# Loading order, constant matmuls and the issue order of a convolution's first stage in a two-layer decoder trunk

## The chip, the cores and the metric

The kernel runs on one core of one Trainium2 chip. The metric is the device time of one execution in microseconds (us). Before the change three runs took 1135.62, 1135.75 and 1136.22 us; the median is 1135.75 us.

A core has five engines with instruction queues of their own, each executed in order: TensorE (PE, matmuls; its weight loads are shown apart as PEld), VectorE (DVE), ScalarE (ACT), GpSimd (POOL) and SyncE (SP, which here only issues DMAs). They wait for one another through semaphores.

## What is computed

Two layers over 512 tokens of 1024 channels, in float32. The part that the change touches is the first half of layer 0; the rest follows behind it.

```python
h = x + conformer_conv(rmsnorm(x, norm_mix[0]), ...)      # layer 0
h = h + swiglu_ffn(rmsnorm(h, norm_ffn[0]), ...)
# shared K/V, windowed attention with sinks, output projection, second SwiGLU, final rmsnorm

def conformer_conv(x, w_pw1, b_pw1, w_dw, b_dw, ln_g, ln_b, w_pw2, b_pw2):
    a = jax.nn.glu(x @ w_pw1 + b_pw1, axis=-1)            # 1024 -> 2 x 1024
    y = depthwise_causal_conv(a, w_dw) + b_dw             # 31 taps for each channel
    y = jax.nn.silu(layernorm(y, ln_g, ln_b))             # statistics over the channels
    return y @ w_pw2 + b_pw2
```

## The kernel before

**Layout and order of the stages.** Activations lie with channels on the partitions: `h` is eight tiles (ct 0 to 7) of 128 channels by 512 tokens. Layer 0 works in two halves of 256 tokens (`HALF[0]`, `HALF[1]`). The first stage runs, for each half and each ct, the first pointwise projection (`Pw1`, two groups of eight f32 matmuls of 128x128 by 128x256, L535: linear part and gate part), the GLU gate (`gate`: a sigmoid on ACT, L544 or L547, and a product on DVE, L549, into the padded tile `apad`), and the 31 taps of the depthwise conv. Then come layer norm and silu (`rows`, the tile `z`), the second projection (`pw2`, L252, f32), and the FFN (`ffn_part`). From the FFN on a weight is split into a high and a low part (L202 on ACT, L203 on DVE) and each product takes three matmuls (L254 to L256). The conv of the second half of the tokens runs beside `pw2` and the FFN of the first half.

**Loads.** SP issues in program order: the first half of the tokens in four pieces of 256 KB (L279), both 512 KB pieces of the first projection weight `w1[0]` (L283), the tap weights `wdw` (L288), the second half of the tokens, then `w1[1]` to `w1[7]`, and later the stream of all other weights in chunks of 512 KB (L186).

**The first norm.** ACT squares the eight token tiles (L321), POOL adds them (L325), TensorE sums over the channels (`step1`, L335), DVE and POOL make the reciprocal root (L337, L339), ACT puts it on a diagonal (L347), and TensorE spreads it over all partitions with a matmul by ones (`spread`, L360). The first `N_RAW` = 2 projections use tokens that are scaled by the gain alone (L510 on DVE, `raw`) and are multiplied by the reciprocal root afterwards in `gate` (L546, L548); the others wait for `norm_x` (L517 on DVE), which writes normalised tokens `xg`.

**The conv.** A class `Half` holds one half. `taps` makes the taps of one ct: the first `TAPS - n_pool` ones on DVE (L582, L584), the last `n_pool` as a product on ACT (L574, L576, into a ring of eight tiles `pr`) and a running sum on POOL (L577); a last POOL add joins both (L587). `N_POOL` says how many go to POOL, for each half and each pair of tiles. `conv` walks over pairs of tiles, one step being one DVE tap of both with the ACT and POOL taps that fall to it. `shift_rows` (L604) makes a common shift from the first pair by two matmuls, which DVE adds (L611). `squares` (L613, ACT) and `sums` (L622, four matmuls by ones for each pair) gather the layer norm's statistics. `scales` copies them (L627, ACT), makes rows (L630, TensorE), mean and reciprocal root (L632, L639), and diagonals (L644, ACT); `spread` (L648) spreads them; `rows` makes `z` (L660, L661 on DVE, L662 on ACT).

**What sets the order of the work.** The tile framework schedules: it takes the program's order as a priority and puts each engine's instructions in a fixed order when the program is built, hoisting what is ready. `tc.issue_after(ins)` holds what is issued inside it behind an instruction. The hand-written part is a loop over the 14 projections that are left after the first two (`projs`, index `at_`): after projection `at_` the conv of the first half is advanced so that it is done at `at_` = 11, the entries of `follow` place statistics (`squares` at 4, 6, 9, 11, `sums` one later, `scales` at 12), and `spread` stands between the two halves of the last projection. At `at_` = 12 the second half's conv is begun with `N_EARLY` = 10 steps (L733 ff.). What is left of it is a paced job: `pace` spreads its steps evenly over the next 44 weight chunks (those of `pw2` and of the FFN's first part).

## Time and profile before

| | us |
|---|---|
| median of three runs | 1135.75 |
| the profiled execution | 1136.61 |
| its span in the profile | 1134.8 |
| TensorE matmul busy, of the span | 1104.5 (97%) |
| TensorE weight loads busy | 961.7 (85%) |
| DVE busy | 666.1 (59%) |
| ACT busy | 513.3 (45%) |
| POOL busy | 341.4 (30%) |
| mean granted clock of TensorE | 0.995 |

The span runs from the first to the last instruction in the record; the execution's time is taken around it and is 1.8 us longer. Busy shares are means over the whole span: in the first 250 us, where the conv runs, DVE, ACT and POOL are much busier than here. The rows of a timeline give start and length in us, engine, line, operation, output and inputs, shape and count, and in square brackets the idle time before and what ended it. One f32 matmul appears as two records. The rows of a stretch `A:B` give its length, then for PE, PEld, DVE, ACT and POOL busy time with the number of instructions begun in brackets, then the granted TensorE clock, the mean busy share of the DMA engines and GB/s.

### The profile page before, as it was taken

The numbers are of one execution on the slowest core, as the hardware profiler recorded it, in microseconds if no ns is written. First come the engines' busy times: TensorE is split into PE (matmuls) and PEld (weight loads), VectorE is DVE, ScalarE is ACT, GpSimd is POOL, SyncE is SP. The second block draws the span as 40 slices with busy tenths as digits, with TensorE's granted clock in tenths as the row PEclk, the third lists the DMA queues.
The fourth block names the chain that finished last, engine by engine and source line by source line (L and its number), as shares of the span: only waits on it lengthen the run. The fifth ranks groups of instructions, "written<-read, shape, count | busy, mean of one in ns | idle before, by whom it ended". The sixth has DMA issues, their size and how long they took to land.

```text
span 1134.8 us, 16051 instructions
## 1 busy us (share of the span) xinstructions
PE 1104.5 (97%) x6126; PEld 961.7 (85%) x6126; DVE 666.1 (59%) x1071; ACT 513.3 (45%) x898; POOL 341.4 (30%) x437
## 2 busy tenths in 40 slices
PE   6999999899999999999999999999999999999997
PEld 5888789899999998888878778888888888888886
DVE  3998748897876643454464675764454333444455
ACT  2786887744654432232352574653332222222234
POOL 2997989921011001121220242332111100110014
PEclk9999999999999999999999999999999999999998
DMA  9380044456555552223323211113323332233232
GB/s 358 112 95 1 0 149 149 130 188 237 171 188 184 186 186 93 93 93 108 96 75 106 81 38 38 38 56 109 96 93 94 102 101 93 93 99 104 95 97 89
DMA packets 41577, 128.16 MB, mean 113 GB/s; under 512 B 4475, under 2 KB 12828, under 8 KB 41500
## 3 DMA queue, kind: packets, MB, share of 16 engines
q1 hardware_dynamic: 40924, 126.69, 35.9%
q8 instruction: 48, 0.79, 0.3%
q10 hardware_dynamic: 576, 0.44, 0.1%
q14 instruction: 29, 0.24, 0.1%
HBM read 121.87 MB, written 5.24 MB: 112 GB/s over the span
## 4 chain that ended last, share of the span: by engine, by line
PE 84%; POOL 5%; DVE 4%; issue 3%; ACT 3%; DMA 0%; SPq 0%; POOLq 0%; ACTq 0%; DVEq 0%
PE bank L254 24%; PE bank L255 24%; PE bank L256 24%; PE bank L535 8%; POOL pr L577 3%; PE bank L864 1%; DVE wlo L203 1%; DVE quad L368 1%; PE bank L885 1%; ACT whi L202 1%; ACT pr L576 1%; PE bank L622 1%; DVE bank L584 1%; DMA h<-in_xT_dram 0%; ACT z L662 0%
## 5 line engine op out<-in xcount | busy, mean ns | idle before, releaser
L255 PE MATMUL bank<-quad,whi 128*128 128x512 f32 (+1 forms) x1584 | 543.4, 343 | 2.0 <-DVE quad L368 2.0
L256 PE MATMUL bank<-quad,wlo 128*128 128x512 f32 (+1 forms) x1584 | 542.4, 343 | 2.4 <-DVE wlo L203 2.4
L254 PE MATMUL bank<-quad,whi 128*128 128x512 f32 (+1 forms) x1584 | 543.0, 344 | 0.2
L203 DVE TENSOR_TENSOR wlo<-raw,whi 128x1024 fp32r<-128x1024 f32 x200 | 272.6, 1363 | 316.8 <-ACT whi L202 306.2
L202 ACT CAST whi<-raw 128x1024 fp32r<-128x1024 f32 x200 | 209.3, 1048 | 338.4 <-PE bank L255 295.8
L255 PEld LDWEIGHTS bank<-quad,whi 128*128 128x128 f32 x1584 | 300.7, 190 | 37.6 <-DVE quad L368 2.7
L256 PEld LDWEIGHTS bank<-quad,wlo 128*128 128x128 f32 x1584 | 300.2, 190 | 38.1 <-DVE wlo L203 3.4
L254 PEld LDWEIGHTS bank<-quad,whi 128*128 128x128 f32 x1584 | 300.4, 190 | 36.5 <-ACT quad L903 0.6
L445 POOL TENSOR_TENSOR tmp<-tmp,tmp 128x512 f32<-128x512 f32 x32 | 45.6, 1426 | 426.7 <-DVE tmp L444 412.2
L577 POOL TENSOR_TENSOR pr<-pr,pr 128x256 f32<-128x256 f32 x208 | 158.6, 798 | 7.5 <-ACT pr L576 6.5
L535 PE MATMUL bank<-quad,w 128*128 128x256 f32 x512 | 116.4, 388 | 8.4 <-DMA w<-in_W_dram 8.4
L535 PEld LDWEIGHTS bank<-quad,w 128*128 128x128 f32 x512 | 99.2, 195 | 23.3 <-DVE quad L510 8.3
L576 ACT ACTIVATE pr<-apad,wdw 128x256 f32<-128x256 f32 x208 | 102.1, 504 | 36.4 <-POOL pr L577 27.6
L584 DVE SCALAR_TENSOR_TENSOR bank<-apad,wdw,bank 128x256 f32<-128x256 f32 x248 | 114.7, 485 | 4.1
L325 POOL TENSOR_TENSOR tmp<-tmp,tmp 128x256 f32<-128x256 f32 (+1 forms) x42 | 44.8, 1066 | 121.9 <-ACT tmp L321 100.5
L443 ACT ACTIVATE tmp<-tmp 128x512 f32<-128x512 f32 x32 | 20.1, 632 | 86.4 <-DVE tmp L442 86.4
L878 POOL TENSOR_SCALAR sc<-sc,sm 128x256 f32<-128x256 f32 (+1 forms) x64 | 30.8, 503 | 86.1 <-DVE sm L876 86.0
L371 ACT CAST quad<-tmp 128x512 fp32r<-128x512 f32 (+1 forms) x60 | 35.3, 592 | 43.5 <-POOL tmp L445 25.8
L372 DVE TENSOR_TENSOR quad<-tmp,quad 128x512 fp32r<-128x512 f32 (+1 forms) x60 | 40.0, 671 | 3.2 <-ACT quad L371 3.2
L437 POOL TENSOR_TENSOR tmp<-tmp,tmp 128x512 f32<-128x512 f32 x12 | 19.7, 1644 | 72.1 <-DVE tmp L433 55.5
L368 DVE SCALAR_TENSOR_TENSOR quad<-h,prm,quad 128x512 fp32r<-128x512 f32 (+1 forms) x40 | 39.4, 1017 | 2.2 <-ACT quad L367 2.0
L444 DVE TENSOR_TENSOR tmp<-bank,rsbc 128x512 f32<-128x512 f32 x32 | 22.1, 691 | 30.4 <-PE bank L256 30.4
(129 smaller groups left out, 754.2 us busy)
## 6 DMA issues: line engine op xcount, KB each, us to landing
raw<-in_W_dram SPq DMA_DIRECT2D x208, 512.0 KB, 3.6
w<-in_W_dram SPq DMA_DIRECT2D x16, 512.0 KB, 9.4
fd<-fs SPq DMA_DIRECT2D x1, 3072.0 KB, 33.8
h<-in_xT_dram SPq DMA_DIRECT2D x8, 256.0 KB, 6.4
bias<-fd SPq DMA_DIRECT2D x8, 256.0 KB, 6.3
out_dram<-res SPq DMA_DIRECT2D x13, 128.0 KB, 1.8
out_dram<-res ACTq DMA_DIRECT2D x3, 128.0 KB, 2.4
wdw<-in_wdw_dram SPq DMA_DIRECT2D x1, 124.0 KB, 6.1
```

The lines of the kernel that those rows point to most:

```text
L202: nc.scalar.copy(hi, r)
L203: lo_engine[0].tensor_sub(lo, r, f32(hi))
L254: nc.tensor.matmul(out, w[0], x[0], start=start, stop=False)
L255: nc.tensor.matmul(out, w[0], x[1], start=False, stop=False)
L256: nc.tensor.matmul(out, w[1], x[0], start=False, stop=stop)
L325: self.eng.tensor_add(sq, self.acc, sq)
L368: nc.vector.scalar_tensor_tensor(dst[1], src, g, f32(dst[0]), op0=ALU.mult, op1=ALU.subtract)
L445: nc.gpsimd.tensor_mul(t2, t1, t2)
L535: mm = nc.tensor.matmul(self.pb[:, w * W2:(w + 1) * W2], w1[ct][:, w, k, :], x[k] if x else xg[k][:, tok], start=k == 0, stop=k == KT - 1)
L576: on_act = nc.scalar.mul(pr, a[:, j:j + W2], tap(j))
L577: nc.gpsimd.tensor_add(pr, acc, pr)
L584: on_dve = nc.vector.scalar_tensor_tensor(yt if i == nd - 1 else c, src, tap(i), c if i else self.shift, op0=ALU.mult, op1=ALU.add)
```

## The change

It does five things. (1) The first tokens and the first half of `w1[0]` are loaded in smaller pieces in the order of use: two token tiles, half of the weights' 512 KB piece, four token tiles, the other half, two token tiles; `wdw` moves from SP's queue to ACT's. (2) Seven 128x128 f32 matmuls of ones by ones are issued ahead of the first projection, into a PSUM bank that nobody reads; POOL sets the ones before the identity, and the table-loading copy on ACT reads a tile that DVE sets. (3) The first norm's row sums are held behind the first projection and its spread goes between the halves of the second. (4) The first half's conv is advanced to be done at `at_` = 10, its last squares, sums and scales come one projection earlier, and the second half's tokens are normalised one projection later. (5) The second half's conv begins with 5, 5, 8 and 4 steps after projections 10 to 13, each portion held behind the last gate's sigmoid and, at 12 and 13, behind the copy of the sums and the diagonals; its POOL taps go from (8, 18, 18, 18) to (13, 17, 17, 17).

```diff
+N_WARM = 7
-N_POOL = ((13, 13, 12, 12), (8, 18, 18, 18))
+N_POOL = ((13, 13, 12, 12), (13, 17, 17, 17))
...
-    load_x(HALF[0])
-    load_w1(0)
-    nc.sync.dma_start(wdw, wdw_in)
+    warm = small.tile([P, 4], F32, tag="warm", name="warm")
+    nc.vector.memset(warm, 1.0)
+    nc.scalar.copy(warm, warm)
+    for i in range(0, KT, 2):
+        nc.sync.dma_start(hT[:, i:i + 2, HALF[0]], xT[i:i + 2, :, HALF[0]].rearrange("k p s -> p k s"))
+        if i % 4 == 0:
+            nc.sync.dma_start(w1[0][:, 0, i:i + 4].rearrange("p a b -> p (a b)"),
+                              W[CHUNK_AT["pw1", 0]][:, i * P:(i + 4) * P])
+    nc.sync.dma_start(w1[0][:, 1].rearrange("p a b -> p (a b)"), W[CHUNK_AT["pw1", KT]])
+    nc.scalar.dma_start(wdw, wdw_in)
     load_x(HALF[1])
...
-    ident = cpool.tile([P, P], F32, tag="ident", name="ident")
-    make_identity(nc, ident)
     ones_c = cpool.tile([P, 1], F32, tag="ones_c", name="ones_c")
     nc.gpsimd.memset(ones_c, 1.0)
     ones_m = cpool.tile([P, P], F32, tag="ones_m", name="ones_m")
     nc.gpsimd.memset(ones_m, 1.0)
+    idle = bank()
+    for _ in range(N_WARM):
+        nc.tensor.matmul(idle[:, 0:P], ones_m, ones_m, start=True, stop=True)
+    ident = cpool.tile([P, P], F32, tag="ident", name="ident")
+    make_identity(nc, ident)
...
-    N_EARLY = 10
+    N_EARLY = (5, 5, 8, 4)
...
-                on_pool = nc.gpsimd.tensor_add(yt, yt, acc)
                 self.last = on_act.ins, on_dve.ins, on_pool.ins
+                nc.gpsimd.tensor_add(yt, yt, acc)
...
         first = [Pw1(0, 0, raw)]
-        rms0.step1()
-        pb0 = norm_x(rms0, HALF[0])
-        nc.scalar.copy(rms0.bc[:, HALF[0]], pb0)
-        first += [Pw1(0, ct, raw) for ct in range(1, N_RAW)]
+        with tc.issue_after(first[0].last[1]):
+            rms0.step1()
+        pb0 = []
+
+        def spread0():
+            pb0.append(rms0.spread())
+            return rms0.spread_mm
+
+        first.append(Pw1(0, 1, raw, mid=spread0))
+        norm_x(rms0, HALF[0], pb0[0])
+        nc.scalar.copy(rms0.bc[:, HALF[0]], pb0[0])
...
-        follow = {1: [rms1.step1], 2: [table], 3: [lambda: norm_x(rms1, HALF[1]), h0.shift_rows]}
-        for p, at_ in enumerate((4, 6, 9, 11)):
+        follow = {2: [rms1.step1, table], 4: [lambda: norm_x(rms1, HALF[1]), h0.shift_rows]}
+        for p, at_ in enumerate((5, 7, 9, 10)):
...
-        follow[12].append(h0.scales)
+        follow[11].append(h0.scales)
...
-            while done < n_taps * min(1, (at_ + 1) / 12):
+            while done < n_taps * min(1, (at_ + 1) / 11):
...
-            if at_ == 12:
-                h1 = Half(1, h0.last)
-                second = h1.background()
-                for _ in range(N_EARLY):
-                    next(second)
...
+            if at_ == 10:
+                h1 = Half(1, h0.last)
+                second = h1.background()
+            if at_ >= 10:
+
+                with ExitStack() as st:
+                    for ins in (gated, h0.copied if at_ == 12 else None, h0.spreads if at_ == 13 else None):
+                        if ins is None:
+                            continue
+                        st.enter_context(tc.issue_after(ins))
+                    for _ in range(N_EARLY[at_ - 10]):
+                        next(second)
+                        early += 1
...
-        job(second, h1.n_steps - N_EARLY, base, base + 44)
+        job(second, h1.n_steps - early, base, base + 44)
```

`gated`, `copied` and `spreads` name the last gate's sigmoid, the copy in `scales` and the last diagonal.

## The prediction

> **What bounds the kernel now.** I read the busy shares and the chain that ended last first (the page's parts 1 and 4).
>
> ```profile
> PE 1104.5 (97%) x6126; PEld 961.7 (85%) x6126; DVE 666.1 (59%) x1071; ACT 513.3 (45%) x898; POOL 341.4 (30%) x437
> ...
> PE 84%; POOL 5%; DVE 4%; issue 3%; ACT 3%; DMA 0%; SPq 0%; POOLq 0%; ACTq 0%; DVEq 0%
> ```
>
> TensorE sets the end. The change adds it seven small matmuls and removes none, so a gain can come only from its 30.3 us of idle time (1134.8 less 1104.5) and from stretches at a lower clock. Next I looked at TensorE's own timeline at the start (start, length, instructions; each f32 matmul is two records, "passes" below).
>
> ```profile
> 8.38 1.19 PE L535 MATMUL bank<-quad,w 128*128 128x256 f32 x2 [8.38 <-DMA w<-in_W_dram]
> 10.45 1.01 PE L335 MATMUL bank<-ones_c,tmp 128*128 128x1 f32 x4 [0.88 <-POOL tmp L325]
> 11.33 9.72 PE L535 MATMUL bank<-quad,w 128*128 128x256 f32 x30
> 20.89 0.59 PE L360 MATMUL bank<-tmp,ones_m 128*128 128x256 f32 x2
> 21.32 20.88 PE L535 MATMUL bank<-quad,w 128*128 128x256 f32 x96
> ```
>
> The first weights land at 8.38. One matmul later the row sums (L335) stand in TensorE's order and block it until POOL's sum of squares is done. Then 30 passes take 9.72 us, while the 96 later ones take 20.88 us, 0.216 us each. The stretches of the timeline, with granted clock, say why:
>
> ```profile
> 11.33:17.41 6.08, 6.08 (x15) 4.86 (x16) 0.16 (x1) 0.69 (x2) 0.72 (x1) 1.00 1.04 407
> 17.41:20.89 3.48, 3.48 (x18) 3.04 (x17) 0.00 (x0) 0.00 (x0) 0.00 (x0) 1.00 1.02 406
> ...
> 174.43:177.84 3.41, 3.41 (x14) 3.23 (x15) 3.38 (x8) 3.35 (x9) 3.41 (x6) 0.50 0.32 121
> 177.84:180.00 2.16, 2.16 (x16) 2.01 (x14) 2.09 (x4) 1.33 (x3) 2.16 (x3) 1.00 0.00 0
> ```
>
> The first number in brackets counts matmul starts. Before 17.41 a pass takes about 0.42 us, after it 0.216: a half clock, though the clock column, which has no record that early, says 1.00. A second half-clock stretch, 0.50 in the column, lasts from 174.43 to 177.84, just after TensorE had stood still. From 17.41 to 174.43 is 46.0 times 3.41 us, so the clock seems to be decided on a grid of 3.41 us: up after a dense grid step (14.00 to 17.41), down after a half empty one. Last, TensorE's waits from 124 to 240 us (total, times, longest), and POOL (fifth engine) in two stretches there:
>
> ```profile
> PE bank L256 <- DVE wlo L203: 2.4, 4, 1.2
> PE bank L622 <- DVE y L611: 2.3, 2, 1.8
> PE bank L252 <- ACT z L662: 1.7, 1, 1.7
> PE bank L255 <- DVE quad L368: 1.2, 1, 1.2
> PE bank L630 <- ACT tmp L627: 0.7, 1, 0.7
> PE bank L648 <- ACT tmp L644: 0.6, 1, 0.6
> PE bank L622 <- ACT sq L613: 0.3, 1, 0.3
> ```
>
> ```profile
> 180.00:200.00 20.00, 20.00 (x165) 19.86 (x164) 15.47 (x25) 14.33 (x27) 18.37 (x22) 1.00 0.44 137
> 200.00:226.00 26.00, 21.66 (x166) 20.43 (x165) 21.11 (x30) 19.86 (x35) 25.41 (x24) 1.00 0.42 135
> ```
>
> These 9.2 us fall where the second half's conv runs on DVE, ACT and POOL beside TensorE: 2.9 from 128 to 144, 1.7 from 172 to 175, about 4.5 from 201 to 222, with POOL full.
>
> **The change, part by part.** Line numbers are those of before; orders are those in which both programs' instructions stand on each engine.
>
> *A. The front.* Bytes moved in the first 9 us and the seen landings (first tokens 3.9, first weights 8.3) put the new pieces at about: tokens 3.9, 5.6, 6.6, 8.1; half pieces of w1[0] 4.7 and 7.4; its second 512 KB 9.6. The seven constant matmuls need only ones_m (memset ends at 1.1 on POOL). A 128-wide f32 pass isn't in the trace; the nearest rows are L335's 1-wide ones (1.01 us for four, pitch 0.21) and 256-wide ones (0.42). I take 0.21, half of the wide one: 14 passes end at 4.1, beside nothing. At 0.42 they would end at 7.0 and delay the first real matmul by 2.3 us. That one comes at 4.8 (0.6 us of DVE, L510, after tokens). At half clock a matmul (0.85 us) is slower than DVE (0.615), so TensorE stays dense from 4.8; the first wholly dense grid step ends between 8.2 and 11.6. At 8.2: 8 slow passes, 24 fast ones (5.2), first projection done at 13.4; at 11.6: 16 and 16, 15.1. The middle is 14.3, plus 0.4 for the row sums (now behind the projection), 32 passes (6.9) and the spread (0.43): 22.0 for the third projection. Before it starts at 21.32 + 6.91 = 28.2. **Gain 6.2**, bounds 5.3 and 7.2. If the row sums' chain is late, the second projection's first half (3.46 us) hides it: DVE 0.16, POOL 0.72, ACT 0.69. w1[1] (13.5, after 3.8 MB at 400 GB/s) isn't late either. wdw goes to ACT's queue: 0.43 us of issue before the first squares, which wait for tokens until 3.9; on SP's queue seven issues still stand ahead of the second tokens, so all later loads keep their places. The identity, made later on POOL, is first read at about 16, and ACT's table load, now behind a DVE memset, ends long before 3.9: both cost nothing, and no more than their own 0.3 us if they were not covered.
>
> *B. First half's statistics.* Squares, sums and scales come one projection (6.9 us) earlier; 10.4 us instead of 3.5 lie between scales and spread. That ends L648's 0.57; L630's 0.70 stays, since sums and row sums still stand back to back. What is late next: in the new order the second half's shift and one sum stand before the first pw2 matmul, with DVE's add between them. DVE does 11 operations for z first (0.37 us each from the spread), so TensorE waits about 0.6 there; the 1.67 for z mostly goes, since this moves pw2 back while z is being made (0 to 1.67 may be left; I take 0.4). 2.94 less 0.70, 0.6 and 0.4: **gain 1.2**, bounds -0.5 and 2.2.
>
> *C. Start of the FFN.* Before, TensorE took the second half of x after 24 matmuls (2.9 us) and met L368 and L611: 1.7 us, then 3.41 us at half clock, a loss of 1.7. In the new order 48 matmuls (5.7 us) use tiles that are ready, against 5.2 us from pw2's end (167.96) to L368's end (173.2), and the first sums stand earlier. All of it is 3.4. The new first lo parts stand on DVE behind pair 1's y, which POOL gives at about 156, so they land about as TensorE comes (161 to 164): I leave 0.8. **Gain 2.6**, bounds 0 and 3.4.
>
> *D. 201 to 222.* Between one pair's sums and the next TensorE had 217 matmuls of 0.119 us (25.8), POOL 38 operations of 0.798 and 2.25 products (L437, 1.64): 34.0. POOL was over by 8.2. With 22 steps done early instead of 10, and 17 POOL taps instead of 18, the new order has 269 matmuls (32.0) against 36 and 2.8: 33.3. Over by 1.3, so a seventh of 4.5 should stay; ACT's and DVE's waits hang on POOL's ring of pr. I take **3.5**, bounds 0 and 4.5.
>
> Behind 240 nothing changes sides: 47 matmuls (5.6 us) instead of 60 cover the second half's chain from L632 to L644's last (274.3 to 278.8, 4.6 us).
>
> Sum: 6.2 + 1.2 + 2.6 + 3.5 = 13.5 us. The profiled execution took 1136.61 (span 1134.8), so 1123.1 for it; it lies 0.86 above the median of 1135.75, from which the forecast is **1122.3**.
>
> The Trainium skill, "TensorE: Matmul & The Clock Gate", Part 1, states that the gate opens after one busy window of about 3.4 us, that the window is free-running, and its closing table asks for at least 4 us of matmuls to warm up. By that rule the constants' 3.0 us are too short alone; the trace agrees on the window (3.41) and no run here shows what 3 us do. If they counted, the clock would be full at the first real matmul.
>
> **Rivals.**
> 1. *The constants open the clock.* Against: from 10.58 to 14.00 a grid step held 0.75 us of 1-wide and 2.7 us of dense matmuls and did not open it. If 80% is enough, DVE's eighth product (9.3) sets the pace and the second projection waits for w1[1] at 13.5: A is 7.4, the time 1121.1. With every upper bound 1118.3.
> 2. *DVE, ACT and POOL keep the second half.* POOL is full from 180 to 226; if the earlier start only shifts this queue, C and D stay: A + B = 7.4, so 1128.4.
> 3. *The first conv falls behind.* Its taps start only 3.5 us earlier (27.3 against 30.8, after the new gates), while TensorE comes to the last sums 13.1 earlier (112.8 against 125.9). Squares then are done at 109.3, 3.5 before; if DVE loses 7, A shrinks by 3.5, and C and D are gone: 1131.9.
> 4. *Slower:* the second half's first pair stands ahead of pw2 in TensorE's order. Before, its y was complete at 158.4 after a start at 113, 45 us. With 45 us from 105 it would come at 150, TensorE stands from 130.4, and the half clock adds 1.7: 19.6 + 1.7 - 13.5 = 7.8, so 1143.5; slower from 144 on. Against: in the new order DVE and POOL do only this pair then: 36 taps of 0.485 and gates, about 20 us.
> 5. Parts cancel and nothing shows: 1135.75.
>
> **How the numbers follow.** Forecast 0.60 (1119.5 to 1125.5), rival 1 0.10, rival 2 0.17, rival 3 0.06, rival 4 0.05, rival 5 0.02. The range takes in the forecast and rivals 1 and 2 with the upper bounds: 1118.5 to 1129.0. A measurement tells apart about 0.2% (2.3 us): faster 0.93, same 0.02, slower 0.05.
>
> **What would show it.** A: L535's third group starts near 22 and the clock is full between 8 and 12. B: no wait at the spread, a short one at the first L622-like sum before pw2. C: no clock at 0.50 after pw2. D: under 1.5 us of waits on lo parts and y. Wrong: a TensorE wait of over 3 us on the first half's sums or ahead of pw2, or a total wait from 160 to 225 as before.

## The result, and the profile after

The changed kernel takes **1139.73 us** (median of seven runs, 1137.72 to 1139.97), the kernel before 1135.75 (seven runs, 1135.12 to 1136.42): a ratio of 1.003, 95% interval 1.002 to 1.0039. It is slower by 4 us where 13.5 us of gain were forecast, and outside the range. The profiled execution of the changed kernel is its fastest one, 1137.72 with a span of 1135.9, so its trace shows some 2 us less loss than the median.

The page of the changed kernel, busy times and the two lines of the chain that ended last:

```profile
PE 1109.7 (98%) x6140; PEld 964.1 (85%) x6140; DVE 669.7 (59%) x1068; ACT 513.1 (45%) x902; POOL 344.1 (30%) x441
...
PE 75%; DVE 7%; issue 5%; POOL 5%; ACT 4%; DMA 2%; SPq 0%; POOLq 0%; ACTq 0%; DVEq 0%
PE bank L255 24%; PE bank L256 24%; PE bank L257 24%; POOL pr L585 5%; DVE bank L592 4%; ACT pr L584 1%; PE bank L888 1%; DMA sk<-in_sinks_dram 1%; DVE wlo L204 1%; PE bank L909 1%; DMA w<-in_W_dram 1%; DVE quad L376 1%; ACT whi L203 1%; DMA h<-in_xT_dram 1%; POOL y L596 0%
```

TensorE's busy time rose by 5.2 us, of which the constants are 3.4. Its share of the chain fell from 84% to 75%: more of the chain runs through the conv's own lines (POOL's adds 5% where it was 3%, DVE's taps 4% where it was 1%), and some through one load that no step of the prediction had priced, `sk<-in_sinks_dram`. (Line numbers of the changed kernel are above those of before, by 1 at the weight splits and by 8 in the conv: L203 is now L204, L577 is L585, L622 is L630. In some of the kernels below they are one or two higher still.)

The start on TensorE is as the change meant it, and better than I had forecast:

```profile
1.02 3.36 PE L307 MATMUL bank<-ones_m 128*128 128x128 f32 x14 [1.02 <-POOL ones_m L304]
4.73 1.10 PE L543 MATMUL bank<-quad,w 128*128 128x256 f32 x4 [0.35 <-DMA w<-in_W_dram]
6.31 7.65 PE L543 MATMUL bank<-quad,w 128*128 128x256 f32 x28 [0.48 <-DVE quad L518]
13.80 0.50 PE L343 MATMUL bank<-ones_c,tmp 128*128 128x1 f32 x4
```

The 32 passes of the first projection end at about 14, and the third projection starts at 21.58 (forecast: 22.0; before: 28.23). The trace's record of the clock is at full from 4.54 on, where before it began at 17.42.

What that lead became is read by taking the time at which TensorE starts the same instruction in each trace. The second column is a time, the others are differences from it in us (the kernels other than the changed one are explained below):

| TensorE starts | before | changed | front_only | front_sk | after_sk |
|---|---|---|---|---|---|
| third projection | 28.23 | -6.64 | -4.57 | -6.53 | -5.59 |
| ninth projection | 74.08 | -6.66 | +2.87 | -6.20 | -7.42 |
| first pass of `pw2` | 138.13 | -1.97 | +3.38 | -5.41 | -4.54 |
| 49th pass of `pw2` | 150.53 | +1.35 | +3.39 | -5.41 | -4.96 |
| 97th split matmul | 186.24 | +0.04 | +1.80 | -5.46 | -2.22 |
| 169th split matmul | 195.50 | +4.39 | +3.35 | -5.42 | +2.18 |
| 601st split matmul | 257.16 | +1.68 | +3.35 | -5.42 | -0.56 |
| last split matmul | 1122.35 | +1.64 | +3.30 | -5.46 | -0.57 |

In these kernels nothing changes behind the 601st split matmul; everything is decided in the first 260 us. Two things have to be known to read the table. First, each column is one execution: before_sk and loop_only, which begin like the kernel before, start the third projection 1.50 and 0.83 us ahead of it, so differences of that size say little. The traces of front_only and after_sk are also 1.4 and 1.6 us longer than those kernels' medians.

Second, the rows compare the same instruction, but not always the same work ahead of it, since parts 4 and 5 move matmuls across these points. In the changed kernel and after_sk one pair's sums (8 passes, 1.7 us) come behind the ninth projection and no longer ahead of it; ahead of `pw2` stand 6 passes more than before (1.3 us), ahead of its 49th pass 12 more (2.6), ahead of the 97th and the 169th split matmul 8 more (1.7). At the third projection and from the 601st split matmul on the work is the same. Counted for equal work, the changed kernel's column reads about -6.6, -4.9, -3.3, -1.2, -1.7, +2.7, +1.7: it has lost 1.7 us by the ninth projection and 3.7 more by the middle of `pw2`, and loses 3.9 between there and the 169th split matmul, ending 1.7 behind. TensorE's waits from 124 to 240 us in the changed kernel (total, times, longest), the counterpart of the list that the prediction shows:

```profile
PE bank L257 <- DVE wlo L204: 3.7, 5, 1.2
PE bank L368 <- ACT tmp L355: 2.7, 1, 2.7
PE bank L630 <- ACT sq L621: 1.3, 1, 1.3
PE bank L253 <- ACT z L670: 1.0, 2, 0.5
PE bank L256 <- DVE quad L376: 0.8, 2, 0.5
PE bank L612 <- POOL y L596: 0.7, 1, 0.7
```

With two smaller ones they sum to 10.9 us, where before it was 9.2; the wait for the FFN's diagonals (L368 on L355) is new. And the clock fell three times instead of once, at 144.49, 178.62 and 195.69, each time for one step of 3.41 us. Two of the three steps, and the stretch between them:

```profile
178.62:182.04 3.42, 3.42 (x15) 3.15 (x15) 3.35 (x6) 2.58 (x5) 3.42 (x4) 0.50 0.03 8
182.04:195.69 13.65, 10.94 (x86) 10.56 (x85) 9.65 (x15) 8.81 (x17) 13.65 (x17) 1.00 0.49 147
195.69:199.10 3.41, 3.41 (x18) 3.41 (x18) 2.84 (x4) 2.50 (x6) 3.41 (x4) 0.50 0.25 48
```

The fifth engine column is POOL: 13.65 of 13.65 us. TensorE ran 86 matmuls in a stretch that has room for 115 (0.119 us each). (The numbers in brackets count the instructions that run in a stretch, not those that begin in it: one that crosses a border counts on both sides.)

Now to the load in the chain. ACT's timeline of the changed kernel:

```profile
21.86 1.03 ACT L329 ACTIVATE tmp<-h 128x256 f32<-128x256 f32 x3
22.90 1.28 ACT L555 ACT_TABLE_LOAD   x1
24.20 0.91 ACT L555 ACTIVATE tmp<-tmp,prm 128x256 f32<-128x256 f32 x2
32.26 0.22 ACT L720 ACTIVATE sk<-sk 128x16 f32<-128x16 f32 x1 [7.15 <-DMA sk<-in_sinks_dram]
32.38 0.71 ACT L329 ACTIVATE tmp<-h 128x256 f32<-128x256 f32 x2
32.99 0.58 ACT L582 ACTIVATE pr<-apad,prm,wdw 128x256 f32<-128x256 f32 x1
```

The two gates' sigmoids (L555) are done at 25.1. Then ACT stands for 7.15 us at L720, a negation of 128x16 numbers that are first read at 266.6: it sits in `table`, and the scheduler put it here. Its load is issued by SP at 21.31, behind the 14 weight pieces, and lands at about 32.2. Behind it in ACT's order wait the squares of the second tokens (L329) and the conv's first product (L582). The same place in the kernel before:

```profile
27.52 0.60 ACT L574 ACTIVATE pr<-apad,prm,wdw 128x256 f32<-128x256 f32 x1 [0.55 <-DVE apad L549]
...
31.09 0.22 ACT L712 ACTIVATE sk<-sk 128x16 f32<-128x16 f32 x1 [1.34 <-DMA sk<-in_sinks_dram]
```

There the conv's first product (L574) stood ahead of it, and ACT came to it late and waited 1.34 us. The load lands at nearly the same time in both (31.1 and 32.2), because all later loads kept their places, as the prediction says; the prediction did not ask who waits for them. POOL's first conv add in the changed kernel, and in the kernel before:

```profile
35.21 0.73 POOL L585 TENSOR_TENSOR pr<-pr,pr 128x256 f32<-128x256 f32 x1
```

```profile
33.25 1.42 POOL L577 TENSOR_TENSOR pr<-pr,pr 128x256 f32<-128x256 f32 x2
```

TensorE is 6.6 us earlier and POOL's part of the conv 1.96 us later.

### The profile page after: what moved, and what is told of

The parts are those of the page before. It is cut to its first block, busy times and chain, and to the rows that moved or that the text cites. A ratio compares the mean times of both kernels' runs of the same rounds, so it can differ in the third digit from the quotient of the medians.

```text
span 1135.9 us, 16119 instructions
## 1 busy us (share of the span) xinstructions
PE 1109.7 (98%) x6140; PEld 964.1 (85%) x6140; DVE 669.7 (59%) x1068; ACT 513.1 (45%) x902; POOL 344.1 (30%) x441
## 3 DMA queue, kind: packets, MB, share of 16 engines
HBM read 121.87 MB, written 5.24 MB: 112 GB/s over the span
## 4 chain that ended last, share of the span: by engine, by line
PE 75%; DVE 7%; issue 5%; POOL 5%; ACT 4%; DMA 2%; SPq 0%; POOLq 0%; ACTq 0%; DVEq 0%
PE bank L255 24%; PE bank L256 24%; PE bank L257 24%; POOL pr L585 5%; DVE bank L592 4%; ACT pr L584 1%; PE bank L888 1%; DMA sk<-in_sinks_dram 1%; DVE wlo L204 1%; PE bank L909 1%; DMA w<-in_W_dram 1%; DVE quad L376 1%; ACT whi L203 1%; DMA h<-in_xT_dram 1%; POOL y L596 0%
## 5 line engine op out<-in xcount | busy, mean ns | idle before, releaser
L204 DVE TENSOR_TENSOR wlo<-raw,whi 128x1024 fp32r<-128x1024 f32 x200 | 277.1, 1386 | 318.3 <-ACT whi L203 309.4
L203 ACT CAST whi<-raw 128x1024 fp32r<-128x1024 f32 x200 | 209.3, 1048 | 344.7 <-PE bank L256 307.4
L585 POOL TENSOR_TENSOR pr<-pr,pr 128x256 f32<-128x256 f32 x212 | 162.9, 801 | 9.9 <-ACT pr L584 9.8
L543 PE MATMUL bank<-quad,w 128*128 128x256 f32 x512 | 113.8, 381 | 1.1 <-DVE quad L518 0.5
L543 PEld LDWEIGHTS bank<-quad,w 128*128 128x128 f32 x512 | 96.5, 190 | 17.2 <-DVE quad L518 3.4
```

The lines of the kernel that those rows point to most:

```text
L203: nc.scalar.copy(hi, r)
L204: lo_engine[0].tensor_sub(lo, r, f32(hi))
L543: mm = nc.tensor.matmul(self.pb[:, w * W2:(w + 1) * W2], w1[ct][:, w, k, :], x[k] if x else xg[k][:, tok], start=k == 0, stop=k == KT - 1)
L585: on_pool = nc.gpsimd.tensor_add(pr, acc, pr)
```

## Experiments

The kernels were formed in groups, each from what the one before had left open. A time is a median; its ratio is to runs of the kernel before on the same chip in the same group (medians 1135.77 to 1136.14). Theory A: the front is worth its 6.6 us, and the early portions of the second half's conv lose them. Theory B: DVE, ACT and POOL hold the second half at their own pace wherever it begins.

### Parts alone

**front_only**: parts 1 to 3, the loop over the projections as before (against the changed kernel, cut).

```diff
-N_POOL = ((13, 13, 12, 12), (13, 17, 17, 17))
+N_POOL = ((13, 13, 12, 12), (8, 18, 18, 18))
...
-        follow = {2: [rms1.step1, table], 4: [lambda: norm_x(rms1, HALF[1]), h0.shift_rows]}
+        follow = {1: [rms1.step1], 2: [table], 3: [lambda: norm_x(rms1, HALF[1]), h0.shift_rows]}
```

> The kernel before with parts 1, 2 and 3 alone (small pieces, constant matmuls, row sums and spread placed); the loop, the statistics and the second half's conv as before. Theory A (the front is worth its 6.6 us, and the earlier portions of the second half's conv lose it again in pw2 and the FFN's start, by TensorE waits and three half-clock stretches): about 1129 us, 6 to 7 below before, the third projection at about 21.6 and the FFN's first split matmul at 162 to 163. Theory B (DVE, ACT and POOL hold the second half whatever is done ahead of it, so that the front's gain ends in waits): 1134 to 1136, the third projection also at 21.6 but the FFN's first split matmul at 167 or later.

Measured: 1137.75 (1137.17 to 1139.16), ratio 1.0018 (1.0009 to 1.0027). Both theories miss the time, and theory A falls: without any of the early portions the front alone is slower than before. TensorE's timeline shows where its lead went:

```profile
39.58 0.61 PE L344 MATMUL bank<-ones_c,tmp 128*128 128x1 f32 x4 [1.94 <-POOL tmp L334]
...
58.75 0.70 PE L613 MATMUL bank<-y,inv_s 128*128 128x256 f32 x2 [3.28 <-POOL y L596]
```

It stands 1.94 us for the squares of the second tokens and 3.28 for the first pair's y, and then runs at half clock from 59.76 to 63.17. ACT stood 5.24 us at the sinks' negation in this kernel (until 32.41). From the ninth projection on the kernel runs 2.9 to 3.4 us behind the one before and keeps that distance nearly everywhere: the whole second half moved with the first.

**loop_only**: parts 4 and 5 with the front of before (against the changed kernel, cut).

```diff
+    load_x(HALF[0])
+    load_w1(0)
+    nc.sync.dma_start(wdw, wdw_in)
...
+        rms0.step1()
+        pb0 = norm_x(rms0, HALF[0])
```

> The kernel before with parts 4 and 5 alone (statistics earlier, second half's conv begun in portions, 13 and 17 POOL taps); loads, first norm and start as before. Theory A: slower than before by about what the changed kernel lost behind its front, 6.6 + 4 = 8 to 11 us, so 1143 to 1147, with half-clock stretches behind pw2's start. Theory B: the loop changes are nearly neutral and the slow part is that the conv can't follow a faster front: within 3 us of before, 1134 to 1139.

Measured: 1139.80 (1138.42 to 1141.13), ratio 1.0033 (1.002 to 1.0045). Between the two theories: parts 4 and 5 lose by themselves, about as much as the whole change.

**no_warm**: the changed kernel without constants.

```diff
-N_WARM = 7
+N_WARM = 0
```

> The changed kernel without the seven constant matmuls. If they opened the clock (full from 4.5 us in the changed kernel's trace, ahead of the first real matmul), the clock now opens between 8 and 12 us and the third projection starts 0.5 to 2 us later, at 22 to 23.5; the time is 1140 to 1142. If the clock opens by the data's own matmuls as early, the third projection stays at 21.6 and the time at 1139.7.

Measured: 1137.62 (1136.64 to 1140.06), ratio 1.0021 (1.0012 to 1.003). The clock was full from 10.67 instead of 4.54, ahead of the first real matmul, so in the changed kernel's execution the constants opened it. The third projection began at 22.56 instead of 21.58. That one pair of executions does not show what the constants are worth: in the 14 traces with them the third projection begins at 21.16 to 23.66, in the two without (this one and front_sk_w0) at 22.56 and 22.10. At the end the kernel without them is 2.1 us the faster by medians, with intervals that overlap; the expectation of 1140 to 1142 was wrong.

**front_stats**: the changed kernel with part 5 undone.

```diff
-    N_EARLY = (5, 5, 8, 4)
+    N_EARLY = 10
...
+            if at_ == 12:
+                h1 = Half(1, h0.last)
```

> The changed kernel with part 5 undone (second half's conv begun with 10 steps after projection 12, POOL taps 8 and 18), so the front and the earlier statistics. Theory A with the portions as the cost: 1128 to 1130, a little faster than the front alone, since the wait of 0.6 at the spread goes. If the earlier statistics are what costs (the first half's conv pressed into one projection less): 1133 or more, with waits on the first half's y or squares.

Measured: 1139.43 (1138.83 to 1139.74), ratio 1.0031 (1.002 to 1.0043). That is the second case of the expectation, and TensorE meets one large wait:

```profile
122.19 1.87 PE L638 MATMUL bank<-ident,tmp 128*128 128x1 f32 x8 [6.76 <-ACT tmp L635]
```

The copy of the sums (L635) stands on ACT behind products of the second half, each of which waits for a slot of the ring `pr` that POOL empties one add at a time. A late POOL thus reaches TensorE by way of an instruction that has nothing to do with POOL.

### One ACT instruction moved

Theory C, from these traces: ACT's stand at the sinks' load starts the conv's products late, POOL is full from its first add on, and its lateness comes back at whatever TensorE waits for next. The test moves the negation behind the first half's statistics. In the traces of all four pairs (before_sk, front_sk and after_sk here, stats_sk below, each against its kernel without the move) it is the only instruction that stands elsewhere: ACT's other instructions and all of DVE, POOL and TensorE keep their order.

```diff
-            nc.scalar.mul(sk, sk, -1.0)
...
+        with tc.issue_after(h0.copied):
+            nc.scalar.mul(sk, sk, -1.0)
```

**before_sk**: this alone in the kernel before.

> The kernel before, with one ACT instruction moved: the negation of the attention's sinks (128x16, in `table`), which waits for a small load at the end of the loads, stands behind the copy of the first half's sums and no longer ahead of the first conv's products. Theory C: ACT's wait for that load is what the front's gain ran into (7.15 us of ACT standing still in the changed kernel, 25.1 to 32.26, and POOL starts the conv at 35.2), and POOL, full from there on, carries the delay to the FFN. In the kernel before ACT waits only 1.34 us there, and TensorE has no wait in the first conv, so C expects little: 1134.0 to 1136.0. Theory B (DVE, ACT and POOL hold the second half by their own pace, wherever it begins): 1135.5 to 1136.2.

Measured: 1135.51 (1134.92 to 1135.87), ratio 0.9993 (0.9984 to 1.0003): no difference that can be told, as expected by both theories.

**front_sk**: this in front_only.

> The front-only kernel (parts 1 to 3, 1137.75 us) with the same one ACT instruction moved. Theory C: POOL begins the first conv some 6 us earlier, so TensorE's waits for the second tokens' row sums (1.94), for the first pair's y (3.28) and the half clock behind them (1.7) go: 1129.5 to 1132.0, faster than before by about 5. Theory B: the same load decides nothing, 1136.0 to 1138.0.

Measured: **1130.42** (1129.88 to 1130.85), ratio 0.9947 (0.9934 to 0.996). One instruction of 0.22 us turns a loss of 0.2% into a gain of 0.5%; theory B does not allow that. ACT and POOL in its trace:

```profile
24.31 0.91 ACT L556 ACTIVATE tmp<-tmp,prm 128x256 f32<-128x256 f32 x2
25.13 0.71 ACT L330 ACTIVATE tmp<-h 128x256 f32<-128x256 f32 x2
25.74 0.58 ACT L583 ACTIVATE pr<-apad,prm,wdw 128x256 f32<-128x256 f32 x1
```

```profile
27.97 0.73 POOL L586 TENSOR_TENSOR pr<-pr,pr 128x256 f32<-128x256 f32 x1
```

POOL's first conv add comes at 27.97, 5.3 us ahead of before and 7.2 ahead of the changed kernel. TensorE has no wait of 0.45 us or more between the first projection and 121 us, and the column of the table stays between -5.4 and -6.6 from the third projection to the end.

**after_sk**: this in the changed kernel.

> The changed kernel with the same one ACT instruction moved. Theory C: TensorE's waits for the first pair's y (1.3 us at 58 to 60) go, but POOL then meets the hold of the second half's portions behind the copy of the sums and the diagonals (POOL stood still from 116.5 to 123.2 in the changed kernel), which swallows most of what it gained: 1136.0 to 1138.5, 1 to 3 below the changed kernel. Theory B: 1139 to 1140, as the changed kernel.

Measured: 1133.94 (1131.13 to 1135.73), ratio 0.9977 (0.9967 to 0.9986): 5.8 us below the changed kernel, more than I had allowed. Slower than front_sk, though: parts 4 and 5 together still cost 3.5 us. (The two profiled executions, 1137.72 and 1135.52 us, lie only 2.2 us apart, the one the fastest of its kernel and the other among the slowest, so the traces show less than half of the 5.8.)

**after_sk_nohold**: after_sk with the portions at 12 and 13 held behind the last gate's sigmoid only.

```diff
-                    for ins in (gated, h0.copied if at_ == 12 else None, h0.spreads if at_ == 13 else None):
+                    for ins in (gated,):
```

> The changed kernel with that ACT instruction moved and the portions of the second half's conv at 12 and 13 held behind the last gate's sigmoid only, no longer behind the copy of the sums and the diagonals. Theory C: POOL neither starts late (7 us) nor stands still at 116.5 (6.7 us), so the second half's first pair is there about 10 us earlier and TensorE's waits before the second projection (1.7), for the squares (1.3) and in the FFN (2.7), with two half-clock stretches (1.7 each), go: 1128 to 1132. Against it: the copy may then stand on ACT behind products that POOL paces, as in front_stats (6.76 us of TensorE at the row sums there); then 1136 to 1139. Theory B: 1138 to 1140.

Measured: 1133.91 (1132.10 to 1134.18), ratio 0.9975 (0.9964 to 0.9986). A miss, and no test of the holds: in the two traces the order of instructions is the same on every engine, so the framework puts the portions where they were with or without these holds. Both labels stand for one program (18 runs, 1131.13 to 1135.73), and POOL stands still for 7.34 us at 110 in both. What the second trace does show is how far two executions of one program differ: it starts the 601st split matmul at 253.21, after_sk's at 256.61.

### What part 5 costs

Theory D1: POOL bounds 136 to 233 us, and part 5 leaves it more to do there. The conv's adds on POOL by stretch (length, busy time, number that run in it), in the kernel before and in the changed one:

```profile
113.00:126.00 13.00, 13.00 (x20) 1.00 0.00 1
126.00:160.00 34.00, 25.91 (x39) 1.00 0.24 72
160.00:226.00 66.00, 51.47 (x55) 0.97 0.45 146
226.00:270.00 44.00, 1.79 (x2) 1.00 0.56 182
```

```profile
113.00:126.00 13.00, 5.58 (x9) 1.00 0.00 0
126.00:160.00 34.00, 28.77 (x43) 0.95 0.21 63
160.00:226.00 66.00, 51.54 (x55) 0.95 0.45 145
226.00:270.00 44.00, 7.48 (x8) 1.00 0.59 188
```

The portions were to feed POOL earlier. It made 9 adds from 113 to 126 instead of 20, since ACT's products stood behind the copy of the sums, which waited 2.97 us for TensorE, and a diagonal, which waited 5.17 us for DVE's mean. Begun earlier, the second half's POOL work came later, and into the dearer place: an add takes 0.66 us between 126 and 160, and 0.94 between 160 and 226, where the weights are split. Eight adds run behind 226, where before it was two. What such an add holds up is seen in after_sk, on DVE, POOL and TensorE:

```profile
187.45 0.15 DVE L345 TENSOR_SCALAR ms<-bank 128x2 f32<-128x2 f32 x1
```

```profile
183.05 8.25 POOL L585 TENSOR_TENSOR pr<-pr,pr 128x256 f32<-128x256 f32 x9
191.27 0.70 POOL L347 TENSOR_TENSOR rs<-ms,mhalf 128x2 f32<-128x2 f32 x1
```

```profile
192.75 0.95 PE L368 MATMUL bank<-tmp,ones_m 128*128 128x256 f32 x2 [2.74 <-ACT tmp L355]
```

The mean square for the FFN's norm is there at 187.6. Its root (L347) is queued on POOL behind nine conv adds until 191.27, 3.7 us, and TensorE waits 2.74 for what comes of it.

**stats_sk**: front_stats with the negation moved, that is, parts 1 to 4.

> Parts 1 to 4 (front, and the first half's statistics one projection earlier), the second half's conv begun as before with 10 steps after projection 12, its POOL taps (8, 18, 18, 18), and the sinks' negation moved behind the copy of the sums. It stands between front_sk (1130.4) and after_sk (1133.9), so it says whether part 4 or part 5 costs the 3.5 us between them. Theory D1 (POOL is the bound of 136 to 233 us, and part 5 puts more in front of what the FFN waits for): as front_sk, 1129.5 to 1131.5. Theory D2 (the moved statistics cost: the copy of the sums stands on ACT behind products that POOL paces, 6.76 us of TensorE in front_stats): 1133 to 1136.

Measured: 1130.96 (1130.69 to 1131.46), ratio 0.9956 (0.9943 to 0.9968). As D1 expects, and not to be told from front_sk: part 4 neither gains nor loses, the 6.76 us of front_stats are 1.25 here, and 3.0 of the 3.5 us are part 5 (its interval just overlaps after_sk's). It also repeats the test of the negation: 8.5 us below front_stats.

**after_sk_p14**: after_sk with smaller POOL shares.

```diff
-N_POOL = ((13, 13, 12, 12), (13, 17, 17, 17))
+N_POOL = ((13, 13, 12, 12), (13, 14, 14, 14))
```

> The changed kernel with the sinks' negation moved and three POOL taps of each of the last six second-half tiles given to DVE: (13, 14, 14, 14) for (13, 17, 17, 17). That takes 18 products off ACT and 18 adds (0.7 to 0.9 us each, some 14 us) off POOL, which was full in all of 160 to 226 us of after_sk, and gives DVE 18 taps (some 9 us). Theory D1: POOL's reciprocal root for the FFN (3.7 us late behind nine adds in after_sk) and the ring of products come free, so TensorE's wait for the diagonals (2.7) and part of those for low parts (5.6) go, with a half-clock stretch: 1128.5 to 1131.5. Theory D2: 1133 to 1134.5.

Measured: 1132.17 (1130.82 to 1133.04), ratio 0.9964 (0.9951 to 0.9976). Half of what D1 hoped for, and its interval overlaps that of after_sk: the wait for the diagonals fell from 2.7 to 1.5, that for low parts from 5.6 to 3.7, and a new one of 1.7 stands at the second half's spread (L656 on L652).

**front_sk_p16**: front_sk with `(8, 16, 16, 16)`.

> front_sk with the second half's POOL taps (8, 16, 16, 16) for (8, 18, 18, 18): 12 adds less on POOL, 12 taps more on DVE. POOL has only 2.3 us of idle time from 170 to 226 us there. D1: some of the 4.0 us of TensorE's waits between 196 and 218 go: 1128.0 to 1130.0. D2: 1130 to 1131. If DVE (17.5 of 20 us busy from 180 to 200, all of 226 to 250) becomes the bound instead: 1131 to 1133.

Measured: 1140.77 (1140.19 to 1141.95), ratio 1.0043 (1.0029 to 1.0057). The third possibility of the expectation, at far more than its price. At the 601st split matmul the kernel is 3.0 us ahead of front_sk, of which 1.7 are one pair's sums that it has still to do; then TensorE comes to the last pair's sums:

```profile
271.23 1.22 PE L631 MATMUL bank<-y,ones_m 128*128 128x256 f32 x2 [6.26 <-POOL y L596]
```

It waits 6.26 us, since DVE's last taps of that pair end at 270.8, and the clock stays at half for four steps. Twelve taps from POOL to DVE move the bound from the one to the other.

**front_sk_w0**: front_sk with `N_WARM = 0`.

> front_sk without the seven constant matmuls. In the two kernels where the constants could be seen alone (changed kernel and no_warm) the third projection began at 21.58 with them and 22.56 without. If no later wait takes it back, now that TensorE waits little in the first conv: 1130.9 to 1131.9, 0.5 to 1.5 slower than front_sk. If the clock opened by the constants is worth nothing: 1130.0 to 1130.8.

Measured: 1131.03 (1130.79 to 1131.41), ratio 0.9956 (0.9944 to 0.9969). It starts the third projection 0.4 us later and ends 0.6 later; the intervals of the two ratios overlap. With no_warm, where leaving them out was 2.1 us to the good, no worth of the constants at the end is shown either way.

### The early begin, the half clock, the last pair

**after_sk_p18**: after_sk with the old shares, `(8, 18, 18, 18)`.

> after_sk with the old shares of the second half's taps, (8, 18, 18, 18) for (13, 17, 17, 17): part 5's early begin without its new shares. POOL has 4 adds less in all (about 3 us), 10 less in the first pair and 6 more in the other three. Theory D1 (POOL's backlog between 136 and 233 us sets the waits): its backlog at 190 us is smaller by about 5 to 8 adds since the first pair is behind it, so 1131 to 1133. If the early begin itself costs, by putting conv adds ahead of the FFN's reciprocal root on POOL: 1133 to 1135.

Measured: 1135.45 (1133.18 to 1136.07), ratio 0.9991 (0.9982 to 1.0). Slower than after_sk by 1.5 (the intervals just overlap): the new shares do not cost, if anything they help. The early begin itself is what costs: with the same shares stats_sk takes 4.5 us less. With smaller shares in the first pair POOL has made its adds of the first portions sooner and stands still for 10.1 us ahead of 118.3, against 7.3 in after_sk. TensorE waits 0.93 instead of 2.74 for the diagonals, and later 3.02 us, at 224.41, for a pair's y.

**after_sk_fill**: after_sk with the wait for the diagonals filled.

```diff
+            for _ in range(fill):
+                nc.tensor.matmul(pb[:, 0:P], ones_m, ones_m, start=True, stop=True)
             nc.tensor.matmul(pb, ones_m, self.diag, start=True, stop=True)
```

> after_sk with ten 128x128 f32 matmuls of ones by ones directly ahead of the FFN's first spread, into the bank that the spread then writes. TensorE waited 2.74 us there for ACT's diagonals and ran the 3.41 us behind it at half clock. Ten constants take about 2.4 us at full clock, so they fit into the wait. If the half clock comes from the wait being empty, 1.7 us goes: 1131.5 to 1133.0. If the clock falls for another reason, or the filling delays the spread: 1133.5 to 1135.

Measured: 1135.13 (1132.51 to 1136.99), ratio 0.999 (0.9981 to 0.9998). The filling went into the wait as it should, and nothing was gained:

```profile
188.31 2.39 PE L369 MATMUL bank<-ones_m 128*128 128x128 f32 x20
191.62 0.70 PE L370 MATMUL bank<-tmp,ones_m 128*128 128x256 f32 x2 [0.91 <-ACT tmp L355]
```

The spread comes 1.1 us earlier than in after_sk and no step of that execution runs at half clock. But the low parts cost 6.6 us of waiting between 160 and 240 instead of 5.6, and 1.1 more goes at 198 for the copy of the spread (L362). Not all of this is the constants' doing: with the edit the framework also put some instructions of ACT, DVE and POOL in another order. At the 601st split matmul after_sk, after_sk_fill and after_sk_p18 come at 256.61, 256.51 and 256.46, with two, no and two half-clock steps, as if time won on the clock were waited off. The other execution of after_sk's program speaks against a rule: with no half-clock step, and with POOL standing still 2.8 us less from 108 to 170 (10.4 against 13.2), it came there 3.4 us earlier. What the half clock costs while the conv's engines set the pace stays open.

**front_sk_p17**: front_sk with `(8, 16, 17, 18)`.

> front_sk with the second half's POOL taps (8, 16, 17, 18): the second pair as in front_sk_p16, the third half way, the last pair as in front_sk. front_sk_p16 was 3.0 us ahead of front_sk at the 600th split matmul and then waited 6.3 us for the last pair's sum and lost four grid steps of clock. If that is the last pair's share alone: 1127.0 to 1129.5. If DVE's load in the two pairs before it already makes the last pair late: 1131 to 1138.

Measured: 1132.60 (1131.41 to 1134.57), ratio 0.9971 (0.9959 to 0.9983). The last pair's wait is down to 0.5, as expected, but the pair before waits 3.30 us for its y at 206 (1.77 in front_sk), and a lead of 2.0 us at the 601st split matmul, of which 1.7 are again sums still to be done, has become a lag of 1.4 by the 1001st. The time lies in the second range of the expectation.

### The portions and the mean

**after_sk_mv**: after_sk with the portion after projection 11 held on DVE behind the mean of the first half's statistics.

```diff
+                self.meaned = nc.vector.tensor_scalar(mv, pt[:, 0:2], 1.0 / D, None, op0=ALU.mult).ins
...
-                    for ins in (gated, h0.copied if at_ == 12 else None, h0.spreads if at_ == 13 else None):
+                    for ins in (gated, h0.meaned if at_ == 11 else None, h0.copied if at_ == 12 else None, h0.spreads if at_ == 13 else None):
```

> after_sk with the portion after projection 11 held on DVE behind the mean of the first half's statistics, so that 12 of the second half's taps (about 0.5 us each) no longer stand ahead of the mean. Theory D1' (the portions delay the statistics that ACT waits for, ACT's products stand behind that wait, POOL stands still 6.6 us, and its adds come in the FFN instead, where one takes 0.94 us and not 0.68): POOL's standstill falls to 1 to 3 us, 5 to 8 adds more are done by 126, and the FFN's waits shrink: 1129.5 to 1132.0. If POOL's standstill is not what the FFN waits hang on: 1133 to 1135.

Measured: 1131.43 (1129.94 to 1132.38), ratio 0.9959 (0.9946 to 0.9971). The time is as expected (its interval just overlaps after_sk's) and the reason is not. POOL stood still at 110 for 7.34 us as in after_sk, because ACT waits there for the sums themselves, and its next products stand behind their copy (L635). The two rows in after_sk, ACT's and POOL's:

```profile
115.20 0.59 ACT L635 COPY tmp<-bank 128x512 f32<-128x512 f32 x1 [6.08 <-PE bank L630]
```

```profile
118.72 1.42 POOL L585 TENSOR_TENSOR pr<-pr,pr 128x256 f32<-128x256 f32 x2 [7.34 <-ACT pr L584]
```

The mean was late only in the changed kernel. What went are two later standstills of POOL in after_sk, 2.7 us at 135 and 2.8 at 156 to 160 (the second is missing from after_sk_nohold's trace, too). From 113 to 160 POOL ran 53 conv adds, in stretches as above, against 47 and 48 in the two traces of after_sk's program, and none run behind 226, against 7 and 3. TensorE's waits for low parts are 3.0 us from 160 to 240, against 5.6 and 4.7; that for the diagonals stayed (3.2, against 2.7 and 3.1). So the effect goes with POOL's backlog, as D1 says, and not through the instruction that I had named; no run changes the backlog alone.

**after_sk_mv_p15**: the same with `(13, 15, 15, 17)`.

> after_sk_mv with POOL taps (13, 15, 15, 17) for (13, 17, 17, 17): 8 adds less on POOL in the middle pairs, 8 taps more on DVE, the last pair as it was. D1': 1128.5 to 1131.0, the fastest so far if it falls below front_sk's 1130.4. If DVE is late at the last pair, as in front_sk_p16: 1132 to 1137.

Measured: 1131.97 (1131.27 to 1132.37), ratio 0.9965 (0.9952 to 0.9979): no better. The four fastest kernels, front_sk (1130.42), stats_sk (1130.96), front_sk_w0 (1131.03) and after_sk_mv (1131.43), cannot be told apart; all beat the kernel before by 0.4 to 0.5% and the changed kernel by 0.7 to 0.8%. The simplest of them are front_sk, parts 1 to 3 with the negation moved, and front_sk_w0, the same without the constants.

## Why the prediction was wrong

**Two steps failed.** Forecast and measurement lie 17.4 us apart. Of these, 5.8 are a wait that no term had (the changed kernel against after_sk), and 10.8 are B, C and D, which were to bring 7.3 us and cost 3.5 where that wait is out of the way (after_sk against front_sk). A itself was 0.5 too high (5.65 for 6.2).

**The first step** is the one that lets TensorE's lead reach the conv: A was carried to the end as it stood at the third projection. The prediction took the conv's start from DVE ("Its taps start only 3.5 us earlier (27.3 against 30.8, after the new gates)", in rival 3); it looked up neither ACT's first product nor POOL's first add. DVE's row of taps did come earlier, by 4.2 us (26.57 against 30.82). POOL's first add came 1.96 us later, and since POOL is full from there to the first pair's y (26.8 of 27 us busy from 33 to 60), nothing makes that good before TensorE needs that y. The row that would have told it was on ACT's timeline of before: 1.34 us at the sinks' load. ACT came there 4.6 us sooner, the load landed 1.2 us later, and the wait grew by both. front_sk against front_only measures the step by itself: 7.3 us.

**The second step** is that steps issued earlier are done earlier, on which C and D rest; it is taken up there.

**A, the front: 6.2 forecast.** At the third projection it was 6.64 in this execution, inside its bounds. It was lost again in the kernel as changed (front_only +1.7 us at the end against the median of before) and is worth 5.65 once the negation is out of the way. The statement that the constants do not open the clock was wrong and rival 1 right for this execution: the clock was full at 4.54. As little hung on it as rival 1 said: no worth at the end is shown.

**B, the statistics: 1.2 forecast.** TensorE waits 0.67, 0.51 and 0.54 ahead of the first `pw2` matmul and 0.44 a little behind it, where 0.6 and 0.4 were priced, and 1.30 more for the second pair's squares, with a half-clock step behind it. In stats_sk, with POOL in time, it waits 2.47 us from the third projection to the middle of `pw2`, against 2.94 in the kernel before, so the term is 0.5 us there, and nothing that can be told at the end. The waits ahead of `pw2` were the ones that it named, priced too low; the one for the squares it did not name.

**C and D, the FFN: 2.6 and 3.5 forecast.** D counted POOL's work (34.0 against 25.8 us, then 33.3 against 32.0), at the whole kernel's mean of 0.798 us an add where an add takes 0.94 between 160 and 226, and both took for granted that steps issued earlier are done earlier. The portions' products stood behind statistics on ACT, and from 113 to 126 POOL ran 9 adds where it had run 20. The waits for low parts and diagonals rose from 2.4 to 6.4 us together, while those for y fell from 2.3 to 0.5. TensorE's waits from 160 to 225 come to 6.1 us in both kernels, which the prediction had named as a sign of being wrong, and the clock was at half from 178.62, where C had none. Where the sinks are out of the way, parts 4 and 5 cost 3.5 us instead of bringing 7.3.

**The rivals.** Rival 2 had the right engines but only let C and D stay; at 1128.4 it kept a front that was already lost. Rival 3 had the right place, with DVE in ACT's stead and 1131.9. Rival 4, the only slower one, was wrong in its mechanism: the first pair of the second half came at 133.7, not at 150, and TensorE waited 0.67 for it. A POOL that starts late was nobody's case; the chance of 0.05 for slower followed from that.

Open: whether an early begin would gain without POOL's standstill (6.8 to 10.1 us in all kernels with early portions). What POOL waits for is seen: in after_sk, after_sk_nohold, after_sk_fill, after_sk_p14 and loop_only ACT's products stand behind the copy of the sums, which waits for TensorE's last sums, and POOL stands still for 7.33 to 7.35 us. But no run took that copy out of the way. A kernel in which the sums come from TensorE ahead of the first portion wasn't tried. How the standstill leads to each of the FFN's waits is argued from the traces, not tested by itself.

## What to carry to other kernels

When a change makes one engine earlier, look on each in-order queue behind it for the first instruction that waits for something that does not move, above all a small load that no one needs yet: its wait grows by the lead, and a short wait in the profile before is the only sign of it. Issuing work earlier helps the engine that is the bound only if the instructions that feed it are not queued behind a wait; count what that engine has finished by a given time, not what has been issued. Before a difference of a few us between two traces is read as an effect, look at two executions of one program: here they lay 3.4 us apart.

## What the runs showed of the hardware that I had not expected

**Whether 3.4 us of constants open the clock differs from execution to execution.** Half-clock steps lie on a grid of 3.41 us whose phase differs from execution to execution. Of the 14 profiled executions with the 3.36 us of constants, nine have the full clock on record from between 4.54 and 6.76 us, and five from between 8.56 and 10.41; the two without constants have it from 10.01 and 10.67. The phase alone does not decide: a step from 1.73 to 5.14 opened it in front_only and one from 1.74 to 5.15 did not in after_sk_fill, where TensorE stood 0.54 us for the first weights and not 0.39. In the nine the last step ahead of the full clock was 85 to 95% busy; in the five no step up to 7 us was over 85%. It can close again at once: in front_only the step from 5.14 to 8.56 held 42% of busy time (1.98 us of waiting for tokens), and the next ran at half clock. The Trainium skill, "TensorE: Matmul & The Clock Gate", Part 1, says that the window of about 3.4 us is free-running; the traces agree (3.41). Its closing table asks for 4 us of matmuls to warm up; here 3.36 us were enough in nine of 14.

**What a wait costs in clock depends on how it falls on the steps.** In after_sk 2.74 us of waiting left one step 20% busy, and the next ran at half clock. In after_sk_nohold, the same program, the same wait was 3.13 us, lay across two steps (63% and 45% busy), and the clock stayed full. In the first 300 us of the traces each step under 43% busy (by the matmul records) that began at full clock was followed by a half one; between 45 and 79% some were and most were not, so busy time alone does not settle it. That may be part of why one program's runs lie up to 4.6 us apart (1131.13 to 1135.73): of these two executions, the one with two half-clock steps took 1135.52 us and the one with none 1132.13.

**POOL's adds are slower beside the weight splits.** A 128x256 add takes 0.68 us from 40 to 100 us (55.46 us for 82) and 0.94 from 160 to 226, where DVE's low parts (128x1024) are made. Taken one by one in the kernel before, the 28 adds of the second stretch that overlap no low part last 0.77 us on average, the 26 that overlap one 1.20. The Trainium skill, "GPSIMD Engine Reference", section 1, lists the access to SBUF as shared with VectorE, with contention for DVE instructions that have two SBUF inputs; the rows agree, since a low part is made from two (`wlo<-raw,whi`), but no run here takes the splits away from the adds.
